# Softmax blocks of two attention branches turned by VectorE and carried through DRAM, both groups of a branch as one stream of steps

## The chip, the cores and the metric

The kernel runs on one core of a Trainium2 chip. The metric is the device time of one execution in microseconds (us). The engines of the core are named as the profile names them: PE (TensorE, matmuls), DVE (VectorE), ACT (ScalarE), POOL (GpSimd) and SP (SyncE, which here only issues DMAs). SPq and POOLq are the DMA queues that SP and POOL issue into. Each engine works through its own instructions in their order and waits, in place, for what the next one needs.

## What is computed

One decoder layer on 512 tokens of width 1024, in float32: h = RMSNorm(x), a projection of h into the columns of three token mixers and their gates, the mixers, their merge, an output projection and a last RMSNorm. Two of the three mixers are softmax attention with 8 heads of 64: forgetting attention (FoX) with a bias per head and key, and block-sparse attention (MoBA), which at this length sees all keys and adds an ALiBi bias. What the change touches is, per head:

```
logits = q @ k.T * scale + bias          # [512, 512], causal
p = softmax(logits, axis=-1)
out = p @ v
```

The third mixer is an mLSTM in chunked form, which has no softmax.

## The kernel before, in words

A float32 value is held as two float32r parts, `hi` and `lo`, and a product is made of three (in the attention: two) float32r matmuls. PE's order is written by hand. Its main stream are the projections: a `Unit` is 256 columns of a weight matrix, fetched in halves of 512 KB (`fetch`, tile `w_raw`, two buffers), split by ACT into `w_hi` and by DVE into `w_lo` (`load`), and used by 24 matmuls of 512 columns per half (lines 148 to 150). `UNIT` is the columns of one such unit, 48 matmuls.

The side work (attention, mLSTM) is a list of steps that `weave` puts between main matmuls: with `part` p and n steps, step i comes when i/n of p times the stage's main columns are done. The stages after the prologue and the first group's projections are:

- stage 2: projections of FoX group 1 (4 units), side: attention of FoX group 0;
- stage 3: projections of the mLSTM (8 units), side: attention of FoX group 1;
- stage 4: merge of FoX and projections of MoBA group 0 (10 units), side: mLSTM;
- stage 5: projections of MoBA group 1 (4 units), side: attention of MoBA group 0;
- stage 6: merge of the mLSTM (6 units), side: attention of MoBA group 1;
- then the merge of MoBA and the output projection.

A group has four heads, and a head two steps of each kind: an even step has the query blocks of 128 and 256 keys, an odd step those of 384 and 512. `scores` makes the logits on PE (lines 366, 367), takes the row maximum and adds the bias on DVE, exponentiates and scales on ACT (line 383, line 386). `transposes` turns each 128 x 128 block of the result by a PE matmul against the identity into PSUM (line 397) and splits it into `pth` and `ptl` (lines 65, 67). `values` multiplies by v (lines 415, 416). Before the change, step n of the list holds scores n, transposes n-1 and values n-2, and each group has a list of its own.

`make_k` copies both parts of k for each head to the other 64 partitions by two DMAs (tiles `sk_h`, `sk_l`). `row_bcast` spreads a row from DRAM over the partitions by a DMA (tile `bias`), and `add_mask` adds a causal mask on POOL. All these DMAs and the weight fetches are issued by SP in the order in which a scheduler puts them; the same scheduler orders ACT, DVE and POOL.

Of the kernel before, what the change touches and what calls it, by code (L numbers as in the profile page):

```python
# [15 lines left out]
P = 128  # L16
# [7 lines left out]
UC = 256  # L24
EPS = 1e-6
# [18 lines left out]
def hybrid_kernel(ctx: ExitStack, tc: tile.TileContext, x, norm_g, w_in, fox_b_f, mlstm_conv_w,  # L44
# [25 lines left out]

    class Unit:
# [107 lines left out]
    def weave(mains, total, side, part=1.0):  # L179
# [7 lines left out]
        for f in side[done:]:  # L187
# [4 lines left out]
    mask_q = const.tile([P, P], F32, name="mask_q")  # L192
    nc.gpsimd.memset(mask_q, 0.0)
    nc.gpsimd.affine_select(out=mask_q, in_=mask_q, pattern=[[-1, P]], compare_op=ALU.is_ge,
                            fill=NEG, base=0, channel_multiplier=1)
    mask_s = const.tile([P, P], F32, name="mask_s")
    nc.gpsimd.memset(mask_s, 0.0)
    nc.gpsimd.affine_select(out=mask_s, in_=mask_s, pattern=[[1, P]], compare_op=ALU.is_ge,
                            fill=NEG, base=0, channel_multiplier=-1)
    alibi = const.tile([P, S], F32, name="alibi")  # L200
    nc.gpsimd.iota(alibi, pattern=[[1, S]], base=P - S, channel_multiplier=-1,
                   allow_small_or_imprecise_dtypes=True)
    nc.gpsimd.affine_select(out=alibi, in_=alibi, pattern=[[-1, S]], compare_op=ALU.is_ge,
                            fill=NEG, base=S - P, channel_multiplier=1)
# [27 lines left out]
    w_f = const.tile([P, KD, 16], F32, name="w_f")  # L232

    ctx.enter_context(tc.manual_schedule(engines={mybir.EngineType.PE}))
    def gate_rows():
        w_fs = att.tile([P, KD, P], F32R, name="pth", bufs=2)
        nc.vector.tensor_scalar(w_fs, h_hi[:, :, S - P:S].bitcast(F32), 0.0, None, op0=ALU.mult)
# [3 lines left out]
        for k in range(KD):  # L241
            nc.tensor.matmul(fps, w_fs[:, k], hh(k), start=k == 0, stop=False)
            nc.tensor.matmul(fps, w_fs[:, k], hl(k), start=False, stop=k == KD - 1)
        pre, shifted, lg, ones_s = (new_bias() for _ in range(4))
        cum = ev.tile([P, S], F32, name="ev")
        nc.scalar.activation(pre, fps, AF.Copy)
# [43 lines left out]
    def make_k(src, scale, name):  # L290
        res = []
        for e in range(2):
# [6 lines left out]
            nc.sync.dma_start(th[o].bitcast(F32), th[r].bitcast(F32))  # L299
            nc.sync.dma_start(tl[o].bitcast(F32), tl[r].bitcast(F32))  # L300
# [14 lines left out]
    class Group:  # L315


        def __init__(self, g, cq, ck, cv, cz, bias, ys):
            self.g, self.bias, self.ys = g, bias, ys
            self.q, self.k, self.z = [], [], []  # L320
            self.u = {n: Unit(w_in_v, c + g * UC) for n, c in (("q", cq), ("k", ck), ("v", cv), ("z", cz))}
# [33 lines left out]
        def scores(self, n):  # L355
# [6 lines left out]
            for i in (2 * half, 2 * half + 1):  # L362
# [5 lines left out]
                pr = (att.tile([P, S], F32, name="pr", bufs=2) if half else  # L368
                      att.tile([P, 2 * P], F32, name="pr0", bufs=2))
# [19 lines left out]
        def transposes(self, n):  # L389
            half = n % 2  # L390
            pth = att.tile([P, NB, 2 * P], F32R, name="pth", bufs=2)
            ptl = att.tile([P, NB, 2 * P], F32R, name="ptl", bufs=2)
            for ii, pr in enumerate(self.pr.pop(n)):
                i = 2 * half + ii
                tp = ps_t.tile([P, S], F32, name="pt")
                for j in range(i + 1):
                    nc.tensor.transpose(tp[:, j * P:(j + 1) * P], pr[:, j * P:(j + 1) * P], ident)  # L397
                cs = slice(ii * P, ii * P + P)
                split(pth[:, 0:i + 1, cs], ptl[:, 0:i + 1, cs],
                      tp[:, :(i + 1) * P].rearrange("p (j q) -> p j q", q=P))  # L400
            self.pt[n] = pth, ptl

        def values(self, n):
# [6 lines left out]
            last = 2 * half + 1  # L410
            for j in range(last + 1):
# [3 lines left out]
                nc.tensor.matmul(reg, vj, pth[:, j, o0:], start=j == 0, stop=False)  # L415
                nc.tensor.matmul(reg, vj, ptl[:, j, o0:], start=False, stop=j == last)  # L416
# [13 lines left out]
        def side(self):  # L430
            self.pr, self.pt = {}, {}
            steps = []
            for n in range(10):
                if n < 8:
                    steps.append(lambda n=n: self.scores(n))
                if 0 < n < 9:
                    steps.append(lambda n=n: self.transposes(n - 1))
                if n > 1:
                    steps.append(lambda n=n: self.values(n - 2))
            return steps  # L440
# [6 lines left out]
    def add_mask(t, mask):  # L447
        d = new_bias()
        nc.gpsimd.tensor_tensor(d.rearrange("p (a b) -> p a b", b=P), t.rearrange("p (a b) -> p a b", b=P),
                                mask[:, None, :].to_broadcast([P, NB, P]), ALU.add)  # L450
        return d

    def fox_bias(h):
        whole = row_bcast(h)
        return whole, add_mask(whole, mask_q)

    def moba_bias(h):
        t = new_bias()
        nc.gpsimd.tensor_scalar(t, alibi, 2.0 ** -(h + 1), None, op0=ALU.mult)
# [41 lines left out]
    class Mlstm:  # L501
# [51 lines left out]
        def weights(self, m):  # L553
            h, j = divmod(m, NB)
            if j == 0:
                self.nmb = row_bcast(8 + h)
                self.nmd = add_mask(self.nmb, mask_s)
# [14 lines left out]
            wh = att.tile([P, S], F32R, name="pth", bufs=2)  # L572
# [411 lines left out]
```

## Time and profile before

| | us |
|---|---|
| median of 3 runs (605.6 to 606.15) | 605.93 |
| the profiled execution | 605.71 |
| its span, from the first to the last instruction | 603.8 |
| PE busy in it | 594.0 |
| DVE busy | 390.7 |
| ACT busy | 334.2 |
| POOL busy | 50.8 |

The span is 1.9 us shorter than the time of the same execution. Busy shares say which engine could be the limit; where the end is really set is read from the chain of waits and from the waits of each engine. A matmul's own duration is longer than the distance to the next one, because matmuls overlap; what a matmul costs on the path is the distance of their starts.

### The profile page before, as it was taken

The numbers are of one execution on the slowest core, as the hardware profiler recorded it, in microseconds if no ns is written. First come the engines' busy times: TensorE is split into PE (matmuls) and PEld (weight loads), VectorE is DVE, ScalarE is ACT, GpSimd is POOL, SyncE is SP. The second block draws the span as 40 slices with busy tenths as digits, with TensorE's granted clock in tenths as the row PEclk, the third lists the DMA queues.
The fourth block names the chain that finished last, engine by engine and source line by source line (L and its number), as shares of the span: only waits on it lengthen the run. The fifth ranks groups of instructions, "written<-read, shape, count | busy, mean of one in ns | idle before, by whom it ended". The sixth has DMA issues, their size and how long they took to land.

```text
span 603.8 us, 8372 instructions
## 1 busy us (share of the span) xinstructions
PE 594.0 (98%) x3109; PEld 509.2 (84%) x3109; DVE 390.7 (65%) x726; ACT 334.2 (55%) x616; POOL 50.8 (8%) x55
## 2 busy tenths in 40 slices
PE   8999999999999999999999999999999999999995
PEld 7988988888988988888898799888888888888884
DVE  6756667764477954856758856666655564356986
ACT  6555676675656545446536467666555433334555
POOL 3000100000000000010000400000000000001302
PEclk9999999999999999999999999999999999999999
DMA  7337432262142632234323642225322339833833
GB/s 249 104 92 176 113 98 78 87 192 88 53 123 71 174 97 79 69 97 113 88 71 95 197 128 71 71 71 148 96 71 71 87 92 342 206 111 76 142 97 139
DMA packets 59276, 69.75 MB, mean 116 GB/s; under 512 B 4972, under 2 KB 48008, under 8 KB 59236
## 3 DMA queue, kind: packets, MB, share of 16 engines
q1 hardware_dynamic: 56900, 64.76, 36.5%
q0 software_dynamic: 2176, 4.19, 4.3%
q8 instruction: 24, 0.39, 0.3%
q10 hardware_dynamic: 160, 0.27, 0.1%
q14 instruction: 16, 0.13, 0.1%
HBM read 61.68 MB, written 2.14 MB: 106 GB/s over the span
## 4 chain that ended last, share of the span: by engine, by line
PE 94%; DMA 2%; ACT 1%; DVE 1%; issue 1%; POOL 0%; SPq 0%; POOLq 0%; ACTq 0%
PE pj L148 22%; PE pj L150 22%; PE pj L149 22%; PE pj L167 4%; PE pj L169 4%; PE pj L168 4%; PE pt L397 3%; PE po L416 2%; PE sp L367 2%; PE sp L366 2%; PE po L415 2%; DMA x<-in_x_dram 1%; DMA w_raw<-in_w_out_dram 1%; DVE w_lo L94 1%; PE pt L865 1%; PE pt L864 1%
## 5 line engine op out<-in xcount | busy, mean ns | idle before, releaser
L148 PE MATMUL pj<-h_hi,w_hi 128*128 128x512 f32 x480 | 191.3, 399 | 0.5 <-DVE sq__3450 L285 0.3
L150 PE MATMUL pj<-h_hi,w_lo 128*128 128x512 f32 x480 | 187.5, 391 | 0.0
L149 PE MATMUL pj<-h_lo,w_hi 128*128 128x512 f32 x480 | 187.1, 390 | 0.0
L94 DVE TENSOR_TENSOR w_lo<-w_raw,w_hi 128x1024 fp32r<-128x1024 f32 x88 | 109.2, 1241 | 71.0 <-ACT w_hi L93 70.1
L93 ACT ACTIVATE w_hi<-w_raw 128x1024 fp32r<-128x1024 f32 x88 | 93.0, 1057 | 72.9 <-PE pj L149 46.8
L150 PEld LDWEIGHTS pj<-h_hi,w_lo 128*128 128x128 f32 x480 | 90.1, 188 | 19.7
L148 PEld LDWEIGHTS pj<-h_hi,w_hi 128*128 128x128 f32 x480 | 90.3, 188 | 18.1 <-issue 1.7
L149 PEld LDWEIGHTS pj<-h_lo,w_hi 128*128 128x128 f32 x480 | 90.4, 188 | 16.5
L167 PE MATMUL pj<-w_hi,h_hi 128*128 128x256 f32 x192 | 56.1, 292 | 0.5 <-ACT h_hi L65 0.5
L169 PE MATMUL pj<-w_hi,h_lo 128*128 128x256 f32 x192 | 55.0, 286 | 0.0
L168 PE MATMUL pj<-w_lo,h_hi 128*128 128x256 f32 x192 | 54.8, 285 | 0.0
L383 ACT ACTIVATE pr<-pr,nmax 128x128 f32<-128x128 f32 (+1 forms) x64 | 35.6, 557 | 27.8 <-DVE nmax L372 16.8
L67 DVE TENSOR_TENSOR ptl<-pt,pth 128x128 fp32r<-128x128 f32 (+1 forms) x64 | 29.3, 486 | 15.2 <-ACT pth L65 14.8
L167 PEld LDWEIGHTS pj<-w_hi,h_hi 128*128 128x128 f32 x192 | 37.2, 194 | 1.2 <-ACT h_hi L65 0.9
L148 PE MATMUL pj<-y_hi,w_hi 128*128 128x512 f32 x96 | 38.1, 397 | 0.0
L168 PEld LDWEIGHTS pj<-w_lo,h_hi 128*128 128x128 f32 x192 | 37.3, 194 | 0.3
L150 PE MATMUL pj<-y_hi,w_lo 128*128 128x512 f32 x96 | 37.5, 390 | 0.0
L149 PE MATMUL pj<-y_lo,w_hi 128*128 128x512 f32 x96 | 37.4, 389 | 0.0
L169 PEld LDWEIGHTS pj<-w_hi,h_lo 128*128 128x128 f32 x192 | 37.1, 193 | 0.2 <-DVE h_lo L67 0.2
L386 ACT ACTIVATE pr<-pr,rden 128x128 f32<-128x128 f32 (+1 forms) x64 | 33.7, 554 | 3.2 <-DVE rden L385 3.0
L65 ACT ACTIVATE pth<-pt 128x128 fp32r<-128x128 f32 (+1 forms) x64 | 24.9, 427 | 4.0 <-PE pt L397 3.9
L117 POOL DMA_DIRECT2D sum<-in_w_out_dram x8 | 9.8, 1225 | 163.4 <-DMA w_raw<-in_w_in_dram 113.2
(313 smaller groups left out, 905.5 us busy)
## 6 DMA issues: line engine op xcount, KB each, us to landing
w_raw<-in_w_in_dram SPq DMA_DIRECT2D x72, 512.0 KB, 3.9
w_raw<-in_w_branch_dram SPq DMA_DIRECT2D x12, 512.0 KB, 4.3
sum<-in_w_out_dram POOLq DMA_DIRECT2D x8, 512.0 KB, 7.1
bias<-scr SPq DMA_DIRECT2D x12, 256.0 KB, 3.1
sk_h<-sk_h SPq DMA_DIRECT2D x20, 128.0 KB, 2.9
sk_l<-sk_l SPq DMA_DIRECT2D x20, 128.0 KB, 6.0
x<-in_x_dram SPq DMA_DIRECT2D x4, 512.0 KB
xr<-in_x_dram SPq DMA_DIRECT2D x1, 2048.0 KB
```

The lines of the kernel that those rows point to most:

```text
L65: nc.scalar.activation(hi, src, AF.Copy, scale=scale)
L67: nc.vector.tensor_tensor(lo, src, hi.bitcast(F32), ALU.subtract)
L93: nc.scalar.activation(hi, raw, AF.Copy)
L94: (eng or nc.vector).tensor_tensor(lo, raw, hi.bitcast(F32), ALU.subtract)
L148: nc.tensor.matmul(bank, hi[:, kk, cs], act_hi(k), start=k == 0, stop=False)
L149: nc.tensor.matmul(bank, hi[:, kk, cs], act_lo(k), start=False, stop=False)
L150: nc.tensor.matmul(bank, lo[:, kk, cs], act_hi(k), start=False, stop=k == u.nk - 1)
L167: nc.tensor.matmul(reg, act_hi(k)[:, ts_], hi[:, kk], start=k == 0, stop=False)
L168: nc.tensor.matmul(reg, act_hi(k)[:, ts_], lo[:, kk], start=False, stop=False)
L169: nc.tensor.matmul(reg, act_lo(k)[:, ts_], hi[:, kk], start=False, stop=k == KD - 1)
L383: nc.scalar.activation(pr[:, :w], pr[:, :w], AF.Exp, bias=nmax, scale=-1.0, accum_out=den)
L386: nc.scalar.activation(pr[:, :w], pr[:, :w], AF.Copy, scale=rden)
```

## The change

`transposes` no longer uses PE. DVE turns the 32 x 32 blocks of each softmax block inside SBUF, one DMA writes the result of a step to DRAM, four DMAs read it back, one for each 32 partitions, so that the full 128 x 128 transpose arises, and the split into `pth` and `ptl` follows from SBUF, one ACT and one DVE instruction per step instead of two each. `values` reads its moving operand in runs of 32 columns. The two groups of a branch become one list of 16 steps that runs over two stages, with values n-4 instead of n-2 beside scores n; the `part` of stages 2, 3 and 5 changes. While this stream runs (`deep`), the weight fetches go to POOL's queue, and so do all copies of k and all row broadcasts, everywhere. The masks become `affine_select` on POOL, the ALiBi tile is made anew per head on POOL and scaled on DVE, and some tiles share buffers (`pr0` in one buffer, `pth0` and `pth1` in one each).

```diff
-            nc.sync.dma_start(raw, self.view[:, 4 * h:4 * h + 4, self.c0:self.c0 + UC])
+            (nc.gpsimd if deep[0] else nc.sync).dma_start(raw, self.view[:, 4 * h:4 * h + 4, self.c0:self.c0 + UC])
...
-            nc.sync.dma_start(th[o].bitcast(F32), th[r].bitcast(F32))
-            nc.sync.dma_start(tl[o].bitcast(F32), tl[r].bitcast(F32))
+            nc.gpsimd.dma_start(th[o].bitcast(F32), th[r].bitcast(F32))
+            nc.gpsimd.dma_start(tl[o].bitcast(F32), tl[r].bitcast(F32))
...
         def transposes(self, n):
             half = n % 2
-            pth = att.tile([P, NB, 2 * P], F32R, name="pth", bufs=2)
-            ptl = att.tile([P, NB, 2 * P], F32R, name="ptl", bufs=2)
-            for ii, pr in enumerate(self.pr.pop(n)):
-                i = 2 * half + ii
-                tp = ps_t.tile([P, S], F32, name="pt")
-                for j in range(i + 1):
-                    nc.tensor.transpose(tp[:, j * P:(j + 1) * P], pr[:, j * P:(j + 1) * P], ident)
-                cs = slice(ii * P, ii * P + P)
-                split(pth[:, 0:i + 1, cs], ptl[:, 0:i + 1, cs],
-                      tp[:, :(i + 1) * P].rearrange("p (j q) -> p j q", q=P))
+            c = (4 * half + 3) * Q
+            pth = att.tile([P, 4, c], F32R, name=f"pth{half}", bufs=1)
+            ptl = att.tile([P, 4, c], F32R, name=f"ptl{half}", bufs=2)
+            tr = att.tile([P, 4, c], F32, name=f"tr{half}")
+            at = 0
+            for pr in self.pr.pop(n):
+                nj = 2 * half + 1 + (at > 0)
+                nc.vector.transpose(tr[:, :, at:at + nj * Q].rearrange("p b (j k) -> p b j k", k=Q),
+                                    pr[:, :nj * P].rearrange("p (j b k) -> p b j k", b=4, k=Q))
+                at += nj * Q
+            raw = ptl.bitcast(F32)
+            turned = dram.tile([4, Q, 4, c], F32, name=f"turned{half}", bufs=2)
+            nc.sync.dma_start(turned.rearrange("a k b c -> (a k) b c"), tr)
+            for b in range(4):
+                nc.sync.dma_start(raw[b * Q:(b + 1) * Q], turned[:, :, b].rearrange("a k c -> k a c"))
+            nc.scalar.activation(pth, raw, AF.Copy)
+            nc.vector.tensor_tensor(ptl, raw, pth.bitcast(F32), ALU.subtract)
...
-                nc.tensor.matmul(reg, vj, pth[:, j, o0:], start=j == 0, stop=False)
-                nc.tensor.matmul(reg, vj, ptl[:, j, o0:], start=False, stop=j == last)
+                for t in (pth, ptl):
+                    if j == last:
+                        src = t[:, :, n0 + j * Q:n0 + (j + 1) * Q]
+                    else:
+                        src = bass.AP(t.tensor, t.offset + j * Q, [t.ap[0], [n0, 2], t.ap[1], [1, Q]])
+                    nc.tensor.matmul(reg, vj, src, start=j == 0 and t is pth, stop=j == last and t is ptl)
...
+    def attention(groups):
+        steps = [[], []]
+        for n in range(16 + DEEP):
+            at = steps[n > 7]
+            for late, name in ((0, "scores"), (1, "transposes"), (DEEP, "values")):
+                if 0 <= n - late < 16:
+                    g, i = divmod(n - late, 8)
+                    at.append(lambda f=getattr(groups[g], name), i=i: f(i))
+        return steps
...
-        nc.sync.dma_start(t, scr[row:row + 1, :].partition_broadcast(P))
+        nc.gpsimd.dma_start(t, scr[row:row + 1, :].partition_broadcast(P))
...
-    weave(fox[1].mains("vzqk"), 4 * UNIT, fox[0].side(), 0.85)
-    weave(mlstm.mains(m_order), 8 * UNIT, fox[1].side(), 0.6)
+    side_a, side_b = attention(fox), attention(moba)
+    weave(fox[1].mains("vzqk"), 4 * UNIT, side_a[0], 0.95)
+    weave(mlstm.mains(m_order), 8 * UNIT, side_a[1], 0.52)
+    deep[0] = False
     weave([merge_a.main()] + moba[0].mains("vqkz"), 10 * UNIT, mlstm.side(), 0.75)
-    weave(moba[1].mains("vzqk"), 4 * UNIT, moba[0].side(), 0.85)
-    weave([merge_c.main()], 6 * UNIT, moba[1].side())
+    deep[0] = True
+    weave(moba[1].mains("vzqk"), 4 * UNIT, side_b[0], 0.95)
+    weave([merge_c.main()], 6 * UNIT, side_b[1], 1.0)
```

How this moves instructions is shown at three places. The first is PE late in stage 3, before: the scores of the last head's odd step, the transposes of its even step, and the values that follow (`po`), with the main matmuls (`pj`) between them left out.

```order
L366 MATMUL sp_2046<-sk_h_1414,sq__1285 128x512
L367 MATMUL sp_2046<-sk_l_1415,sq__1285 128x512
...
L397 MATMUL pt_2074<-ident_87,pr0_1955 128x128
L397 MATMUL pt_2078<-ident_87,pr0_1966 128x128 x2
...
L415 MATMUL po_2015<-pth_1985,v_683 128x256
L416 MATMUL po_2015<-ptl_1986,v_683 128x256
```

The same place of PE in the changed kernel, from the last head's first values on (its even step reads `pth0`, its odd step `pth1`; of the nine and the six main matmuls ahead of them the last one stands).

```order
L358 MATMUL sp_1979<-sk_l_1355,sq__1199 128x512
...
L154 MATMUL pj_2102<-h_hi_98,w_lo_1947 128x512
L424 MATMUL po_2113<-pth0_1998,v_668 128x256
L424 MATMUL po_2113<-ptl0_1999,v_668 128x256
...
L154 MATMUL pj_2102<-h_hi_98,w_lo_1947 128x512
L424 MATMUL po_2113<-pth1_2047,v_668 128x256
L424 MATMUL po_2113<-ptl1_2048,v_668 128x256
```

No PE row is left between scores and values; from the last scores to the odd step's values PE now has 48 main matmuls and the values of four other steps, 8 + 4 + 8 + 4 matmuls.

The second place is SP at the same point of the changed kernel, where before it issued weights, rows and copies of k: `turned` is the block in DRAM, 0 for even and 1 for odd steps, and the last four rows are those of the last head.

```order
L399 DMA turned0_1827<-tr0_1824 128x384
L399 DMA turned1_1922<-tr1_1919 128x896
L401 DMA ptl0_1823<-turned0_1827 32x4x96 x4
L401 DMA ptl1_1918<-turned1_1922 32x4x224 x4
L399 DMA turned0_2003<-tr0_2000 128x384
L399 DMA turned1_2052<-tr1_2049 128x896
L401 DMA ptl0_1999<-turned0_2003 32x4x96 x4
L401 DMA ptl1_2048<-turned1_2052 32x4x224 x4
```

The reads of an even step's block stand behind the write of the next odd step's.

The third place is the queue that carries the copies of k from stage 2 to stage 3. Before, it is SP's:

```order
L444 DMA bias_1540<-scr_118 128x512
L81 DMA w_raw_1305<-in_w_in_dram 128x4x256
L81 DMA w_raw_1370<-in_w_in_dram 128x4x256
L299 DMA sk_h_1384<-sk_h_1384 64x512
L300 DMA sk_l_1385<-sk_l_1385 64x512
```

In the changed kernel the same work stands on POOL, with its own computation between:

```order
L452 DMA bias_1534<-scr_103 128x512
L85 DMA w_raw_1282<-in_w_in_dram 128x4x256
L290 DMA sk_h_1309<-sk_h_1309 64x512
L291 DMA sk_l_1310<-sk_l_1310 64x512
L290 DMA sk_h_1315<-sk_h_1315 64x512
L291 DMA sk_l_1316<-sk_l_1316 64x512
L458 AFFINE_SELECT bias_1536<-bias_1534 128x512
```

All six kinds keep their order; what changed is the engine that issues them. From stage 5 to stage 6 POOL has a `w_raw` fetch between the `sk_h` and the `sk_l` of the first head. POOL issues 50 of the 88 `w_raw` fetches.

## Rows read from the trace of the kernel before

**Rows 1.** The page: engines; the chain that ended last, by engine.

```profile
PE 594.0 (98%) x3109; PEld 509.2 (84%) x3109; DVE 390.7 (65%) x726; ACT 334.2 (55%) x616; POOL 50.8 (8%) x55
...
PE 94%; DMA 2%; ACT 1%; DVE 1%; issue 1%; POOL 0%; SPq 0%; POOLq 0%; ACTq 0%
```

**Rows 2.** All waits of PE: for whom, us, times, longest us.

```profile
PE sp L696 <- DVE idle L691: 1.5, 1, 1.5
PE pj L167 <- ACT h_hi L65: 0.5, 1, 0.5
PE pj L148 <- DVE sq__3450 L285: 0.3, 1, 0.3
```

**Rows 3.** The chain in order of time: start us, us, what.

```profile
69.74 0.33 PE pt L397 x3
...
485.42 0.76 PE pt L397 x7
```

**Rows 4.** Timeline of PE, start us, us: values, main matmuls.

```profile
108.83 0.28 PE L415 MATMUL po<-pth,v 128*128 128x256 f32 x1
...
109.72 0.45 PE L148 MATMUL pj<-h_hi,w_hi 128*128 128x512 f32 x1
...
119.09 0.39 PE L149 MATMUL pj<-h_lo,w_hi 128*128 128x512 f32 x1
...
125.44 0.39 PE L150 MATMUL pj<-h_hi,w_lo 128*128 128x512 f32 x1
```

**Rows 5.** Timeline of one odd softmax step, stage 3.

```profile
176.21 0.34 PE L366 MATMUL sp<-sk_h,sq__1285 128*128 128x384 f32 x1
...
179.28 1.22 ACT L386 ACTIVATE pr<-pr,rden 128x384 f32<-128x384 f32 x2
```

**Rows 6.** DMA issues: xcount, KB each, median us from issue to landing.

```profile
w_raw<-in_w_in_dram SPq DMA_DIRECT2D x72, 512.0 KB, 3.9
...
sum<-in_w_out_dram POOLq DMA_DIRECT2D x8, 512.0 KB, 7.1
bias<-scr SPq DMA_DIRECT2D x12, 256.0 KB, 3.1
sk_h<-sk_h SPq DMA_DIRECT2D x20, 128.0 KB, 2.9
sk_l<-sk_l SPq DMA_DIRECT2D x20, 128.0 KB, 6.0
...
out_dram<-xr SPq DMA_DIRECT2D x6, 256.0 KB, 2.0
```

**Rows 7.** All landings of w_raw; then POOL's DMAs of line 117.

```profile
DMA to landing us min/median/max: 3.3/3.9/9.5
...
L117 POOL DMA_DIRECT2D sum<-in_w_out_dram x8: 1203/1203/1378, 511.4 to 570.1; - x8
...
DMA to landing us min/median/max: 5.9/7.1/9.5
```

**Rows 8.** Timeline: a copy of k at the end of stage 2.

```profile
120.43 0.59 ACT L296 ACTIVATE sk_h<-pj 64x512 fp32r<-64x512 f32 x1 [0.77 <-PE pj L150]
...
121.76 0.46 SPq L300 DMA_DIRECT2D sk_l<-sk_l  x1
```

**Rows 9.** Groups by line: busy us, mean ns, idle before.

```profile
L94 DVE TENSOR_TENSOR w_lo<-w_raw,w_hi 128x1024 fp32r<-128x1024 f32 x88 | 109.2, 1241 | 71.0 <-ACT w_hi L93 70.1
L93 ACT ACTIVATE w_hi<-w_raw 128x1024 fp32r<-128x1024 f32 x88 | 93.0, 1057 | 72.9 <-PE pj L149 46.8
...
L67 DVE TENSOR_TENSOR ptl<-pt,pth 128x128 fp32r<-128x128 f32 (+1 forms) x64 | 29.3, 486 | 15.2 <-ACT pth L65 14.8
...
L622 DVE RECIPROCAL bias<-bias 128x512 f32<-128x512 f32 x1 | 3.4, 3353 | 1.3 <-ACT bias L621 1.3
```

**Rows 10.** Stages 2 and 3: PE, PEld, DVE, ACT, POOL busy, clock, DMA share.

```profile
63.00:125.00 62.00, 62.00 (x374) 54.92 (x374) 42.24 (x117) 42.74 (x91) 6.48 (x5) 1.00 0.34 101
125.00:192.00 67.00, 67.00 (x394) 59.00 (x393) 39.43 (x111) 41.59 (x92) 5.20 (x4) 1.00 0.35 102
```

More of the change, by code (lines that the diff above doesn't have):

```diff
@@ L24 @@
 UC = 256
+Q = 32
+DEEP = 4
 EPS = 1e-6
@@ L367, in scores @@
                 nc.tensor.matmul(sp[:, :w], qs, kl[:, :w], start=False, stop=True)
-                pr = (att.tile([P, S], F32, name="pr", bufs=2) if half else
-                      att.tile([P, 2 * P], F32, name="pr0", bufs=2))
+                if half:
+                    pr = att.tile([P, S], F32, name="pr", bufs=2)
+                else:
+                    if i == 0:
+                        pr0 = att.tile([P, 2, 2 * P], F32, name="pr0")
+                    pr = pr0[:, i]
                 nmax = small.tile([P, 1], F32, name="nmax")
@@ L410, in values @@
             last = 2 * half + 1
+            n0 = last * Q
             for j in range(last + 1):
@@ L428, in values, with add_mask @@
                     self.ys.append(y)
[L430 to L440, printed above, removed]
+    def attention(groups):
[7 more added lines that the diff above has]
+        return steps
     def row_bcast(row):
         t = new_bias()
-        nc.sync.dma_start(t, scr[row:row + 1, :].partition_broadcast(P))
+        nc.gpsimd.dma_start(t, scr[row:row + 1, :].partition_broadcast(P))
         return t
-    def add_mask(t, mask):
+    def add_mask(t, sign):
         d = new_bias()
-        nc.gpsimd.tensor_tensor(d.rearrange("p (a b) -> p a b", b=P), t.rearrange("p (a b) -> p a b", b=P),
-                                mask[:, None, :].to_broadcast([P, NB, P]), ALU.add)
+        nc.gpsimd.affine_select(out=d.rearrange("p (a b) -> p a b", b=P), in_=t.rearrange("p (a b) -> p a b", b=P),
+                                pattern=[[0, NB], [-sign, P]], compare_op=ALU.is_ge, fill=NEG, base=0,
+                                channel_multiplier=sign)
         return d
@@ L454, in fox_bias @@
         whole = row_bcast(h)
-        return whole, add_mask(whole, mask_q)
+        return whole, add_mask(whole, 1)
     def moba_bias(h):
         t = new_bias()
-        nc.gpsimd.tensor_scalar(t, alibi, 2.0 ** -(h + 1), None, op0=ALU.mult)
+        nc.gpsimd.iota(t, pattern=[[1, S]], base=P - S, channel_multiplier=-1,
+                       allow_small_or_imprecise_dtypes=True)
+        nc.gpsimd.affine_select(out=t, in_=t, pattern=[[-1, S]], compare_op=ALU.is_ge,
+                                fill=NEG, base=S - P, channel_multiplier=1)
+        nc.vector.tensor_scalar(t, t, 2.0 ** -(h + 1), None, op0=ALU.mult)
         return t, None
@@ L571, in weights @@
             nc.vector.tensor_tensor(w[:, :n], sp[:, :n], w[:, :n], ALU.mult)
-            wh = att.tile([P, S], F32R, name="pth", bufs=2)
-            wl = att.tile([P, S], F32R, name="ptl", bufs=2)
+            wh = att.tile([P, S], F32R, name=("pth1", "wh")[m % 2], bufs=(1, 1)[m % 2])
+            wl = att.tile([P, S], F32R, name="ptl1", bufs=2)
             split(wh[:, :n], wl[:, :n], w[:, :n])
@@ L581, in weights @@
             if j == NB - 1:
-                self.sums[h] = fold(self.sum, att.tile([P, S], F32R, name="sum_h"))
+                self.sums[h] = fold(self.sum, att.tile([P, S], F32R, name="tr1"))
         def values(self, m):
```

35 lines of the change are left out of this document (13 added, 22 removed).

## Prediction

> **What bounds the kernel now.** I read the page first: PE is busy for 98% of the span and makes up 94% of the chain that ended last [rows 1]. A busy PE alone proves little, so the waits of PE come next: in the whole run there are three, 2.3 us together, two of them in the prologue [rows 2]. From the first projection on PE runs from one matmul into the next, and every other engine's delays are hidden. In the timeline main matmuls of 512 columns start 0.227 us apart (28 of them from 119.09 to 125.44) though each lasts 0.39 [rows 4]. So a matmul taken off PE is worth the distance of starts that it filled, as long as nothing else begins to hold PE up. The kernel is PE's stream, and there are two questions: how much of it goes, and which waits come into it.
>
> **What is removed.** The chain in order of time has the transposes in pieces of three (0.33 us, even steps) and of seven (0.76 or 0.77 us, odd steps), the first at 69.74, the last at 485.42 [rows 3]. Each of 16 heads has one of either: 16 x (0.33 + 0.77) = 17.6 us. That is 0.11 us for each of 160 transposes, and they hide behind nothing, since PE has no gap beside them. I take 17.6.
>
> The Trainium skill weighs the same choice in "VectorE: DVE Perf Modes", section "The three transpose paths": it gives 390 ns to a 128 x 128 transpose on TensorE (2-byte type). By that figure the sum would be an estimated 62 us saved; the row shows 0.11 us apart, because the matmuls overlap, and the row decides.
>
> **What is added off PE.** Per head DVE turns 1280 columns; no row shows its transpose. Below it is bounded by the split of line 94, 1241 ns for 1024 columns, above by the slowest DVE row per column, the reciprocal of line 622, 3353 ns for 512 [rows 9]: 25 us or 134 us in all. The operation reads one operand and writes one, as cheap rows do, so I take 25. The splits that go with it shrink: 64 DVE instructions of 486 ns become 32 over 640 columns on average, at line 94's rate 0.78 each, so 31 becomes 25, and ACT likewise saves a little. Net DVE gains about 5 us per stage, and in stage 2 it is idle for 62.0 - 42.2 = 19.8 us [rows 10]: covered. At the upper bound it would not be (rivals).
>
> The DMAs carry each step's block out and back, 1280 x 512 bytes per head and direction, 21 MB in all, half of it in stages 2 and 3. Over their 129 us that is 81 GB/s more on 101, so their DMA share of 0.34 goes to an estimated 0.62 [rows 10]. No bandwidth bound; but landings may lengthen.
>
> The values now read runs of 32 columns. Their rows show only contiguous reads; an odd step's eight matmuls take 109.72 - 108.83 = 0.89 us, which is the rate of the main ones, and an even step's, with 768 columns in place of 1792, 0.38 [rows 4]. Lower bound of the change: nothing. Upper: the slowest rate per column that PE shows in these stages, that of the transposes, 0.11 us for 128 columns against 0.057, which on 16 x 1.27 = 20.3 us would be 19 more. Nearest is the contiguous read of the same type and size, so I take 0.
>
> **The trip through DRAM, and whom it makes wait.** Nobody but the values waits for it, and DEEP puts them four steps behind the scores. The tightest place is the last odd step of stage 3, where no scores follow to fill the gap: 48 main matmuls (10.9 us), the scores themselves (1792 columns, 0.79) and four steps of values (2 x 0.89 + 2 x 0.38) give 14.2 us from the scores to the values that need them. The chain in that time: scores to scaled softmax 4.3 us (176.21 to 179.28 + 1.22) [rows 5]; turning the last 512 columns 0.62 at line 94's rate; the write to DRAM 2.0 as a store of the output lands; four reads issued 0.46 apart [rows 8], the last 1.4 after the first; landing 2.9, as the copy of k [rows 6]; ACT 0.93 and DVE 1.09 for 896 columns at the rates of lines 93 and 94 [rows 9]. Sum 13.2, one us inside. With reads that land in 6.0 as `sk_l` does [rows 6] the values come 2.1 late; with 9.5, the slowest `w_raw` [rows 7], 5.6, and each handoff and each busy engine comes on top. I take 1 us and keep 0 and 6.6. At the same place of stage 6 the steps are farther apart and the margin is some 5 us: 0. Early and in the middle of the stream the distance is larger: main matmuls worth 86 of 512 columns and five steps of scores, 22.1 us, for the first step, and 26.3 for the first of group 1. SP's order makes an even step's reads wait for the next odd step's write; that adds one step, about 6.5 us, to a chain of 13: still inside.
>
> **What moves to POOL.** The copies of k decide two places. At the end of stage 2 the first head's copies can start when the last matmul of the bank is done; before, ACT starts at 120.43 and SP issues the second copy 1.33 us later [rows 8]. The first scores of stage 3 need it after 21 main matmuls and the values of one odd step, 5.7 us. On POOL an issue takes 1.2 us [rows 7], so the second copy starts at 1.85. If it lands in 2.9, PE does not wait; if in 7.1, as POOL's DMAs do [rows 6], it waits 3.3 us. From stage 5 to 6 a weight fetch stands between the two copies, another 1.2 us, against 24 main matmuls and the same values, 6.3 us: 0 or 3.8. Both ends together 0 to 7.1; I take 2, nearer to the SP row, because it is the same copy of 128 KB, while POOL's rows move 512 KB and add to what is there.
>
> The weights: each of two `w_raw` buffers goes through release, fetch, landing and 1.06 + 1.24 us of split. Call X the time from release to landing; a half can be had every (X + 2.3)/2 us. PE without its transposes uses one in 57.6 / 8 = 7.2 us in stage 2 and, by the main matmuls of the 67 us, 6.4 in stage 3. So X may be 12.1 and 10.5. POOL's median is 7.1 and its slowest 9.5 [rows 7]: covered, and two split halves lie ahead besides. What stands behind a blocked POOL instruction is every fetch and copy after it: `affine_select` waits for the row's landing (3.1 [rows 6]), which brings a slow fetch to 13.8 with its issue. Those are single ones, at most one per head; the two halves ahead absorb them. Masks and ALiBi tiles are off the path: 0.
>
> **Sum**, against the profiled execution's 605.7: -17.6 + 2 + 1 = -14.6, so 591.1; the median of the runs lies 0.2 above that execution, so I say 591. Its own range: 588 without a wait, 602 with both waits at their slow ends.
>
> **Rivals.**
> 1. *POOL supplies the weights too late.* If X is 13.8 throughout stages 2 and 3, a half costs (13.8 + 2.3)/2 = 8.05 us, 0.85 more than PE's in stage 2 (8 halves) and 1.65 in stage 3 (10): 23 us, less the two halves ahead, 13: 10 us, hence 601. For it: 50 fetches stand in one queue with waiting computation. Against: the measured 7.1. The Trainium skill, "SBUF — State Buffer", section "SBUF: two separate sides", speaks against the change here: a DMA from GpSimd's queue has its descriptors written by GpSimd and stalls while VectorE holds the shared port in a two-port operation, 620 ns becoming about 3100. By that figure an estimated X would be 9.6, still short of 10.5; no run here shows it so far. Chance 0.13.
> 2. *The other side: the trip is longer than the four steps.* Place: the reads on SP. With write and reads at 9.5 each the chain is 27.3 us; the distances are 22 to 26. Each window of four steps then loses their difference, 1 to 5 us; eight windows, about 25: 616. It decides from the point where the chain passes some 26 us, because 14.6/8 = 1.8 per window eats the gain. For it: DMA share nearly doubles and reads come in pieces of 384 or 896 bytes. Against: 13 us to spare. Chance 0.07.
> 3. *PE reads runs of 32 columns at half rate*: 591 + 19 = 610, the gain gone and more. Nothing in the trace speaks for it or excludes it. Chance 0.06.
> 4. *DVE turns at the reciprocal's rate*: 33.5 us per stage against 19.8 idle less the 4.4 that PE no longer spends, and similarly in the other three: about 50 us, 641. Chance 0.03.
> 5. *Many small waits at the stage boundaries* that use up the gain; the time unchanged. Chance 0.05.
>
> **How the numbers follow.** 0.66 is left for the forecast. A measurement of this kernel tells about 0.2% (1.2 us) from no change. Faster takes the forecast, nearly all of rival 1 and a little of 5: 0.79; same 0.04; slower, rivals 2 to 4 and what is left, 0.17. The range takes in the forecast's own ends and rival 1, 587.5 to 604, and leaves out 2 to 4.
>
> **What would show it.** Right: PE's chain without line 397 and its busy time about 17 us less; waits of PE for `sk_l` or `sk_h` at the first scores of stages 3 and 6, a few us in all; perhaps one for `ptl` in the last values of stage 3; values at 0.89 us per odd step; DVE's transposes near 0.6 us for 512 columns. Wrong: waits of PE for `w_hi` or `w_lo` (rival 1), for `pth` at every values step (rival 2), values stretched to 1.7 us (rival 3), DVE over 90% busy (rival 4). The forecast fails most easily by the landing of POOL's DMAs, which carries both the copies and the weights.

## The result and the profile after

The changed kernel takes 596.31 us (median of 4 executions, 594.71 to 958.02) against 605.76 (4 executions, 605.11 to 606.15); the ratio is 0.9836, with a 95% interval of 0.9813 to 0.9859. One of the four executions was disturbed (958.02, granted clock 0.558) and is not in the ratio; the median of the other three is 596.01. The profiled execution took 596.01 (its span is 594.2), 9.7 us less than the 605.71 of the one before, where 14.6 were forecast.

The page, engines and chain by engine; the rows answer to [rows 1].

```profile
PE 578.3 (97%) x2949; PEld 493.8 (83%) x2949; DVE 415.6 (70%) x766; ACT 333.5 (56%) x584; POOL 105.0 (18%) x159
...
PE 83%; ACT 4%; DVE 4%; DMA 4%; issue 3%; POOL 1%; SPq 0%; POOLq 0%; DVEq 0%; ACTq 0%
```

PE has lost 160 instructions and 15.7 us of busy time, but its share of the chain fell from 94 to 83%: PE now waits for others. Its waits by line, with total us, times and longest, against the three in [rows 2] (L357 and L358 are the matmuls of the scores, L424 those of the values, L152 to L154 main matmuls):

```profile
PE sp L358 <- DMA sk_l<-sk_l: 2.3, 2, 1.9
PE sp L710 <- DVE idle L705: 1.5, 1, 1.5
PE po L424 <- DVE ev L431: 1.2, 1, 1.2
PE pj L152 <- DVE sq__485 L276: 1.1, 1, 1.1
PE po L424 <- DVE ptl L403: 0.9, 1, 0.9
PE pj L171 <- ACT h_hi L67: 0.7, 1, 0.7
PE po L424 <- ACT pth L402: 0.7, 1, 0.7
PE pj L152 <- DVE sq__3451 L276: 0.3, 1, 0.3
```

No wait is for `w_hi` or `w_lo`, and none for the trip in the middle of the stream. What is new stands at four places: one in the prologue (`sq__485`), one at each first scores of a new group (`sk_l`, stage 3 and stage 6), and three in the last values of stage 3 (`ev`, `pth`, `ptl`). The timeline of PE (start us, us, what, and in brackets the idle time and who ended it) shows what they cost on the path, as the distance of starts:

```profile
43.59 0.39 PE L154 MATMUL pj<-h_hi,w_lo 128*128 128x512 f32 x1
45.05 0.47 PE L152 MATMUL pj<-h_hi,w_hi 128*128 128x512 f32 x1 [1.07 <-DVE sq__485 L276]
...
119.14 0.30 PE L357 MATMUL sp<-sk_h,sq__1149 128*128 128x128 f32 x1
119.86 0.30 PE L358 MATMUL sp<-sk_l,sq__1149 128*128 128x128 f32 x1 [0.42 <-DMA sk_l<-sk_l]
...
153.62 0.28 PE L424 MATMUL po<-pth,v 128*128 128x256 f32 x1
...
154.51 0.33 PE L171 MATMUL pj<-w_hi,h_hi 128*128 128x256 f32 x1
...
169.92 0.39 PE L154 MATMUL pj<-h_hi,w_lo 128*128 128x512 f32 x1
171.53 0.39 PE L424 MATMUL po<-pth,v 128*128 128x256 f32 x1 [1.22 <-DVE ev L431]
...
176.30 0.39 PE L154 MATMUL pj<-h_hi,w_lo 128*128 128x512 f32 x1
177.34 0.38 PE L424 MATMUL po<-pth,v 128*128 128x256 f32 x1 [0.65 <-ACT pth L402]
178.66 0.39 PE L424 MATMUL po<-ptl,v 128*128 128x256 f32 x1 [0.94 <-DVE ptl L403]
...
403.43 0.22 PE L357 MATMUL sp<-sk_h,sq__4091 128*128 128x128 f32 x1
405.50 0.30 PE L358 MATMUL sp<-sk_l,sq__4091 128*128 128x128 f32 x1 [1.86 <-DMA sk_l<-sk_l]
...
407.16 0.63 PE L154 MATMUL pj<-h_hi,w_lo 128*128 128x512 f32 x1
407.59 0.63 PE L152 MATMUL pj<-h_hi,w_hi 128*128 128x512 f32 x1
```

Less the normal distance, the prologue's wait costs 1.46 - 0.23 = 1.2, the first scores of stage 3 0.7 and of stage 6 2.0, and the end of stage 3 1.4 + 0.8 + 1.2 = 3.4 us. Behind the wait of stage 6 seven main matmuls, from 407.16 on, start 0.43 us apart in place of 0.23: another 1.4. That makes 8.7 us of waits, and -17.6 + 8.7 = -8.9 against a measured -9.7.

The remaining 0.8 does not come from a different start: over the profiles of this study PE's first main matmul starts between 8.7 and 9.8 us, but in these two at 9.40 (before) and 9.59 (after), and the last one at 596.09 and 586.62, so it is PE's stream between them that is 9.7 us shorter. Most of the 0.8 lies in the 17.6. Around an even step's transposes in the kernel before:

```profile
80.71 0.40 PE L150 MATMUL pj<-h_hi,w_lo 128*128 128x512 f32 x1
80.95 0.49 PE L397 MATMUL pt<-ident,pr 128*128 128x128 f32 x3
81.19 0.47 PE L148 MATMUL pj<-h_hi,w_hi 128*128 128x512 f32 x1
81.51 0.39 PE L149 MATMUL pj<-h_lo,w_hi 128*128 128x512 f32 x1
...
82.20 0.39 PE L149 MATMUL pj<-h_lo,w_hi 128*128 128x512 f32 x1
```

The three transposes fill 0.24 us to the next start, but the first main matmul behind them is followed only after 0.32. From 80.71 to 82.20 five main matmuls start, at 0.227 each 1.13 us, so the piece costs 0.36. Taken like this over all 32 pieces it is about 0.35 for an even and 0.78 for an odd step, 18.1 us in all, and -18.1 + 8.7 = -9.4; 0.3 us stay open. The values of an odd step, 153.62 to 154.51, take 0.89 us as before [rows 4].

### The profile page after: what moved, and what is told of

It is laid out like the page before. It is cut to its first block, busy times and chain, and to the rows that moved or that the text cites. A ratio compares the mean times of both kernels' runs of the same rounds, so it can differ in the third digit from the quotient of the medians.

```text
span 594.2 us, 8543 instructions
## 1 busy us (share of the span) xinstructions
PE 578.3 (97%) x2949; PEld 493.8 (83%) x2949; DVE 415.6 (70%) x766; ACT 333.5 (56%) x584; POOL 105.0 (18%) x159
## 4 chain that ended last, share of the span: by engine, by line
PE 83%; ACT 4%; DVE 4%; DMA 4%; issue 3%; POOL 1%; SPq 0%; POOLq 0%; DVEq 0%; ACTq 0%
PE pj L152 20%; PE pj L153 19%; PE pj L154 19%; PE pj L171 4%; PE pj L173 4%; PE pj L172 4%; PE po L424 3%; DMA sk_l<-sk_l 2%; PE sp L358 2%; ACT w_hi L97 2%; PE sp L357 1%; DMA x<-in_x_dram 1%; DVE w_lo L98 1%; DVE ptl L403 1%; DMA bias<-bias 1%
## 5 line engine op out<-in xcount | busy, mean ns | idle before, releaser
L152 PE MATMUL pj<-h_hi,w_hi 128*128 128x512 f32 x480 | 189.5, 395 | 1.4 <-DVE sq__485 L276 1.1
L154 PE MATMUL pj<-h_hi,w_lo 128*128 128x512 f32 x480 | 187.8, 391 | 0.0
L98 DVE TENSOR_TENSOR w_lo<-w_raw,w_hi 128x1024 fp32r<-128x1024 f32 x88 | 107.6, 1222 | 64.9 <-ACT w_hi L97 61.8
L152 PEld LDWEIGHTS pj<-h_hi,w_hi 128*128 128x128 f32 x480 | 90.7, 189 | 19.5 <-issue 2.2
L154 PEld LDWEIGHTS pj<-h_hi,w_lo 128*128 128x128 f32 x480 | 90.4, 188 | 19.4
L85 POOL DMA_DIRECT2D w_raw<-in_w_in_dram x44 | 33.8, 769 | 168.9 <-DVE w_lo L98 122.8
L152 PE MATMUL pj<-y_hi,w_hi 128*128 128x512 f32 x96 | 37.9, 395 | 0.0
L394 DVE STREAM_TRANSPOSE tr<-pr 128x128 f32<-128x128 f32 (+1 forms) x64 | 32.2, 506 | 7.6 <-ACT pr L381 6.1
L154 PE MATMUL pj<-y_hi,w_lo 128*128 128x512 f32 x96 | 37.4, 390 | 0.0
L403 DVE TENSOR_TENSOR ptl<-ptl,pth 128x384 fp32r<-128x384 f32 (+1 forms) x32 | 26.7, 833 | 7.0 <-ACT pth L402 6.8
```

Of the source, the lines that this page charges most:

```text
L85: (nc.gpsimd if deep[0] else nc.sync).dma_start(raw, self.view[:, 4 * h:4 * h + 4, self.c0:self.c0 + UC])
L98: (eng or nc.vector).tensor_tensor(lo, raw, hi.bitcast(F32), ALU.subtract)
L152: nc.tensor.matmul(bank, hi[:, kk, cs], act_hi(k), start=k == 0, stop=False)
L154: nc.tensor.matmul(bank, lo[:, kk, cs], act_hi(k), start=False, stop=k == u.nk - 1)
L403: nc.vector.tensor_tensor(ptl, raw, pth.bitcast(F32), ALU.subtract)
```

## The experiments

All are the changed kernel with the edit shown. Times are medians; the kernel before, run beside them, took 604.6 to 605.2. "A" in the expectations was my theory after the first reading: POOL's queue order and DMAs make the copies of k late.

**e1_k_sp.** In `make_k`, both copies:

```diff
-            nc.gpsimd.dma_start(th[o].bitcast(F32), th[r].bitcast(F32))
+            nc.sync.dma_start(th[o].bitcast(F32), th[r].bitcast(F32))
```

> The copies of k are issued by SP again, all else as changed. Theory A (the copies are late because of POOL's queue: issued behind a weight fetch, 0.78 us, and landing in 5 us where SP's took 2.9): PE's two waits for sk_l (0.7 and 2.0 us) and the half clock behind the second (1.7 us) go, 596.0 - 4.4 = 591.6 us. Rival B (the copies land late because the DMA engines carry the trip of the softmax blocks, whoever issues them): landing stays near 5 us, a wait of 1 us or more stays at the first scores of stage 6, 594 us or more.

595.56 us, ratio 0.9837 (0.9814 to 0.986): no better than the changed kernel. The copies land a little earlier (median 4.0 and 3.9 us in place of 4.9 and 5.0), and the wait at stage 6 falls from 1.9 to 1.1 us. So POOL is a part of the lateness and not most of it; A was too simple. Its 2.9 us was also the figure of `sk_h` alone: `sk_l`, for which PE waits, had 6.0 on SP before the change [rows 6]. Rival B's signs came (a wait of over 1 us, 594 us or more), but the cause that it names, the trip's traffic, is tested by e4.

**e2_w_sp.** In `fetch`, `(nc.gpsimd if deep[0] else nc.sync)` becomes `nc.sync`.

> All weight fetches are issued by SP, the copies of k and the rows stay on POOL. Theory A: no fetch stands between the copies of k any more, so sk_l starts 0.8 us earlier at stage 6: the wait there falls from 2.0 to about 1.2, and the prologue's 1.0 us goes; if SP held nothing else this would be 593 us or less. Rival C (SP's order decides: a fetch waits there for a free buffer, up to 12 us on POOL in the changed kernel, and the reads and writes of the trip stand behind it): PE waits for pth or ptl at many values steps, 1 us or more each over 28 steps, 610 us or more.

614.35 us, ratio 1.0152 (1.0122 to 1.0183), slower than the kernel before. SP's own longest wait in total (first fence) and those of PE at the values (second):

```profile
SPq L85 <- DVE w_lo L98: 244.5, 57, 12.5
```

```profile
PE po L424 <- ACT pth L402: 4.5, 4, 1.8
PE po L424 <- DVE ptl L403: 3.7, 4, 1.5
PE po L424 <- DMA w_raw<-in_w_in_dram: 3.0, 1, 3.0
```

A fetch stands on SP until DVE has released its buffer, up to 8.3 us while a stream runs (the 12.5 of the row is in stage 4, and stands in the changed kernel too), and the trip's reads and writes stand behind it. C was right in kind, though PE waits nine times at the values and not at nearly every step: sending the fetches to POOL is what lets the trip through, worth 18 us here. One thing of A held: the prologue's wait fell from 1.1 to 0.2 us, so that one came from the fetch moved to POOL.

**e3_part.** `side_a[1], 0.52` becomes `0.65` (the part of stage 3).

> The part of stage 3 goes from 0.52 to 0.65, so the last four values stand 25% farther apart. Theory A (the three waits of PE at the end of stage 3, 1.38 + 0.81 + 1.21 = 3.4 us, are the last steps following each other too closely, with no scores between): they go or fall below 0.5 us in all, 592.6 us. Rival B (what is late there is the trip itself, and the steps in the middle of the stage have the same chain): waits of 2 us or more stay, 594.5 us or more.

594.27 us, ratio 0.9828 (0.9806 to 0.985). The waits of the last values are now 1.5 for `ptl`, 0.8 for `ev` and 0.2 for `pth`: 2.5 us in place of 2.8. More room between the steps did not remove them; A's figure of 0.5 is refuted. At the first scores of stage 3 a wait of 1.3 us for `sk_h` is new.

**e4_no_trip.** The trip through DRAM is left out, so only the 32 x 32 blocks are turned. After `tr` is made:

```diff
-            raw = ptl.bitcast(F32)
-            turned = dram.tile([4, Q, 4, c], F32, name=f"turned{half}", bufs=2)
-            nc.sync.dma_start(turned.rearrange("a k b c -> (a k) b c"), tr)
-            for b in range(4):
-                nc.sync.dma_start(raw[b * Q:(b + 1) * Q], turned[:, :, b].rearrange("a k c -> k a c"))
-            nc.scalar.activation(pth, raw, AF.Copy)
-            nc.vector.tensor_tensor(ptl, raw, pth.bitcast(F32), ALU.subtract)
+            nc.scalar.activation(pth, tr, AF.Copy)
+            nc.vector.tensor_tensor(ptl, tr, pth.bitcast(F32), ALU.subtract)
```

> The trip through DRAM is left out: pth and ptl are split straight from what DVE turned, so only the 32 x 32 blocks are turned and the output is not the reference's; 21 MB of DMA traffic go, the order on PE stays. Rival B (traffic and length of the trip cause the waits): the waits at the end of stage 3 go and the copies of k land in about 3 us, so their waits and the half clock go too: 596.0 - 3.4 - 4.4 = 588 us. Theory A (order of POOL, ACT and DVE): the copies land as late as before and the wait of 2.0 us with its half clock stays; of the waits at the end of stage 3 the one for the evacuation of po (1.4 us) stays: 592 to 594 us.

594.14 us, ratio 0.9817 (0.98 to 0.9833), an interval that overlaps that of the changed kernel: without 21 MB of traffic and without the trip's latency little is won. The waits of PE that bear on it:

```profile
PE po L419 <- DVE ev L426: 3.5, 3, 2.1
PE sp L358 <- DMA sk_l<-sk_l: 1.8, 2, 1.6
```

With 0.5 us for `sk_h` the waits for k are 2.3 us, as in the changed kernel; the waits for `pth` and `ptl` are gone, but those for `ev` have grown from 1.2 to 3.5, so the values wait no less in all (3.5 in place of 2.8). B falls as the cause of the lost time: PE waits as long without the trip and its traffic. What is left is the order in which ACT and DVE do their work. In the changed kernel ACT shows it at both places (start us, us, what, idle before and who ended it):

```profile
174.62 0.60 ACT L430 ACTIVATE ev<-po 64x512 f32<-64x512 f32 x1 [1.75 <-PE po L424]
175.82 1.06 ACT L97 ACTIVATE w_hi<-w_raw 128x1024 fp32r<-128x1024 f32 x1 [0.60 <-PE pj L153]
176.78 0.50 ACT L402 ACTIVATE pth<-ptl 128x384 fp32r<-128x384 f32 x1
...
393.83 0.59 ACT L275 ACTIVATE sq__4139<-pj 64x512 fp32r<-64x512 f32 x1 [2.53 <-PE sp L358]
...
396.89 1.05 ACT L97 ACTIVATE w_hi<-w_raw 128x1024 fp32r<-128x1024 f32 x1
397.96 0.59 ACT L287 ACTIVATE sk_h<-pj 64x512 fp32r<-64x512 f32 x1
```

At 174.62 the split for the next values (`pth`, 176.78) stands behind the emptying of a bank that waits for PE's own values of the step before. Its data had been there for four us: the four reads of that block were issued before 170.4 and landed within 2.4 us. At 393.83 ACT has stood 2.53 us for the last scores of the old group, which free the buffer of q; the softmax of that step and a weight split follow, and `sk_h` comes at 397.96.

**e5_pe_turn.** PE turns the blocks again, in the changed order and with the changed queues:

```diff
-            pth = att.tile([P, 4, c], F32R, name=f"pth{half}", bufs=1)
...
+            pth = att.tile([P, c], F32R, name=f"pth{half}", bufs=2)
...
-                nc.vector.transpose(tr[:, :, at:at + nj * Q].rearrange("p b (j k) -> p b j k", k=Q),
-                                    pr[:, :nj * P].rearrange("p (j b k) -> p b j k", b=4, k=Q))
-                at += nj * Q
...
+                tp = ps_t.tile([P, S], F32, name="pt")
+                for j in range(nj):
+                    nc.tensor.transpose(tp[:, j * P:(j + 1) * P], pr[:, j * P:(j + 1) * P], ident)
+                split(pth[:, at:at + nj * P], ptl[:, at:at + nj * P], tp[:, :nj * P])
+                at += nj * P
```

> The softmax blocks are turned by PE again, 160 transposes against the identity, with everything else of the change kept: the list of steps over two stages with values four steps behind, POOL's queue for weights, rows and copies of k, the masks. Theory A (the turn off PE is worth 18 us, and the waits come from POOL's queue and from the order of ACT and DVE at the stage borders, whoever turns): the waits of 1.1 us in the prologue and of 2 to 4 us at the first scores of stages 3 and 6 stay, 611 to 614 us, which is 6 us or more above the kernel before. Rival E (the waits come from what DVE and the trip do now): without them they vanish and the time is that of the kernel before, 605 to 608 us.

The trip goes too, and `values` reads contiguous columns again. 607.59 us, ratio 1.0034 (1.002 to 1.0047). All the rest of the change without its core costs 2 us. The waits of PE that bear on it:

```profile
PE sp L358 <- DMA sk_l<-sk_l: 1.3, 1, 1.3
PE pj L152 <- DVE sq__485 L276: 1.0, 1, 1.0
```

A and E each hold in half: the wait for k at stage 6 and that of the prologue stay, whoever turns; that for k at stage 3 and those at the end of stage 3 are gone, so they belong to what ACT and DVE do for the new way. One thing is not kept apart here: the edit also gives `pth` two buffers in place of one. In the changed kernel ACT stands 6.6 us in all for PE before the splits `pth`, at eight of 32; the one at 176.78 is not among them. Turning off PE is worth 607.6 - 596.3 = 11.3 us net: the 18.1 less the 3.4 of the tail, the 1.4 of low clock (no stretch of it here) and about 1 at the copies of k would be 12.3.

**e6_po2.** `self.po = ps_o.tile([P, S], F32, name="po")` becomes `ps_t.tile([P, S], F32, name="pt")`.

> The result of the values gets the two PSUM banks of pt, which the attention no longer uses, in place of the one bank po; one line. Theory A (a step's values wait until ACT and DVE have emptied the bank of the step before, behind the split of the next block): the wait of PE for DVE's ev (1.4 us) goes, and the other two of the tail (0.8 and 1.2 us) move little: 594.6 us. Rival (that wait only hides the late blocks behind it): the same time is waited for pth or ptl instead, 596 us.

594.8 us, ratio 0.9814 (0.9791 to 0.9838), as A expected: the wait for `ev` is gone, 0.9 for `ptl` and 0.6 for `pth` stay. The interval overlaps that of the changed kernel, so the time alone decides nothing; the missing wait does.

**e7_parts.** The parts of stages 2 and 5 back to 0.85, that of stage 3 0.65.

> The parts of stages 2 and 5 go back to 0.85 as they were before the change (from 0.95), that of stage 3 is 0.65. Theory A (the first copies of k are late because ACT and DVE still work on the last softmax step of the stage when the bank of k is done: sk_l is issued 3.2 us after it, 1.5 us before the change): with the last step of stages 2 and 5 some 4 us earlier, sk_h and sk_l are made at once, the copies are issued 1.5 us earlier and the wait at stage 6 falls from 2.0 to 0.5 us or less, the one at stage 3 goes: about 591.5 us with the gain of the wider tail. Rival A2 (it is the 5 us that a copy issued by POOL takes to land): the wait falls by less than 0.7 us, 593.5 us or more.

603.01 us, ratio 0.9964 (0.9952 to 0.9977): most of the gain is lost, the opposite of what I expected. PE waits 8.3 us for `sk_h` at the two borders, 6.3 of them at stage 3. The timeline of POOL there:

```profile
115.88 0.77 POOL L85 DMA_DIRECT2D w_raw<-in_w_in_dram  x1 [1.38 <-DVE w_lo L98]
116.65 0.55 POOL L290 DMA_DIRECT2D sk_h<-sk_h  x1
```

The copy stands behind a fetch that waits for DVE, and then lands after 7.7 us. As I read the timelines (no run takes it apart): with all steps done earlier, PE runs straight from the bank of k to the first scores, and the last values, their emptying and their split now fall on ACT and DVE in just that time. Moving the stage's steps moves the collision, it does not take it away.

**e8_all and e9_four.** e8: copies of k on SP, the parts of e7, the bank of e6, and `deep` set only ahead of stage 2. e9: the same with 0.95 kept in stages 2 and 5.

> All four edits that single runs point to: copies of k on SP, the parts of the run e7_parts, two banks for the values, and weight fetches on POOL only from stage 2 on (not in the prologue, where the fetch on POOL collides with the copy of the gate rows and costs 1.1 us). Theory A: every wait found so far is taken away at its place, 596.0 - 4.4 - 3.4 - 1.1 = 587 us, and the profile shows less than 1.5 us of waits of PE after the prologue. Rival (the waits move to the next place in ACT's or DVE's order): 590 us or more, with new waits named in the profile.

> As the run e8_all, but stages 2 and 5 keep the part of 0.95: copies of k on SP, part of stage 3 0.65, two banks for the values, weight fetches on POOL only from stage 2 on. If the part of 0.85 was what cost e7_parts and e8_all their time (the first scores of the next stage then come while ACT and DVE still hold the block, the bank of the values and the split that stand ahead of k), the gains of the single runs add: 596.3 - 1.0 (prologue) - 1 to 2 (copies) - 2.0 (tail) - 1.5 (bank) = 590 to 591 us. Rival (all these waits are one chain through ACT and DVE, so what one edit saves the next one saves again): 593 us or more.

600.05 us (0.9914, 0.9894 to 0.9935) and 595.24 (0.9839, 0.9814 to 0.9865). In e8 PE waits 2.9 us for `sk_l`, 2.2 for `ptl` and 1.7 for `pth`, in e9 still 2.0, 1.5 and 1.4. The gains of single edits do not add. That fits the rival, one chain through ACT and DVE behind all the waits; the chain itself was not followed in these two.

**e10_kq.** The order of the projections in the second group, in the list of units and in the stages:

```diff
-    weave(fox[1].mains("vzqk"), 4 * UNIT, side_a[0], 0.95)
+    weave(fox[1].mains("vzkq"), 4 * UNIT, side_a[0], 0.95)
...
-    weave(moba[1].mains("vzqk"), 4 * UNIT, side_b[0], 0.95)
+    weave(moba[1].mains("vzkq"), 4 * UNIT, side_b[0], 0.95)
```

> In stages 2 and 5 the projection of k comes before that of q, so that the copies of k have a unit of 11 us more before the first scores of the next stage; all else as changed. Theory L (what PE waits for there is the landing of the copy, 5 us, after a late issue): the two waits (0.7 and 2.0 us, and the half clock of 1.7 us where it follows) go, 592 to 593.6 us. Theory O (what is late there is ACT's and DVE's order, whatever they evacuate): PE now waits for sq by 1 us or more at these two places, 595 us or more.

590.35 us (590.1 to 591.54), ratio 0.9759 (0.974 to 0.9778), below the changed kernel by more than both intervals. All waits of PE of 0.5 us and more:

```profile
PE sp L710 <- DVE idle L705: 1.5, 1, 1.5
PE po L424 <- DVE ev L431: 1.5, 1, 1.5
PE pt L780 <- DVE x L771: 1.2, 1, 1.2
PE pj L152 <- DVE sq__485 L276: 1.1, 1, 1.1
PE po L424 <- DVE ptl L403: 0.9, 1, 0.9
PE po L424 <- ACT pth L402: 0.7, 1, 0.7
```

Nobody waits for k or q at the borders. L holds, O falls: q is just as late on ACT and DVE, but it needs no copy, so it is in time. At the two borders the copies on POOL still take 2.4 to 6.2 us to land; they now have a unit's time for it. The gain, 6.0 us, is more than the 4.1 of the two waits and the half clock in the profile of the changed kernel. Between the two profiles (5.9 us) 1.8 of it comes from the prologue, which the edit does not touch: PE's 26th main matmul starts at 14.14 in place of 15.94. From there on the stream is 4.3 us shorter, 0.9 at the first scores of stage 3, 3.7 at those of stage 6 and -0.3 in the tail.

**e11_kq_three.** e10 with the part of 0.65, the two banks, and `deep` from stage 2 on.

> The projection of k before that of q in stages 2 and 5, with the part of stage 3 at 0.65, two banks for the values, and weight fetches on POOL only from stage 2 on; the copies of k stay on POOL. Theory L: no wait at the borders, none over 1 us in the tail, none in the prologue: 588 to 590 us, below the runs of single edits. Theory O: a wait for sq or pth of 1 us or more at the borders, 592 us or more.

594.65 us (0.9823, 0.9801 to 0.9844): 4 us worse than e10. The prologue's wait is gone, but a new one of 2.0 us for DVE's `nmax` stands at the second scores of stage 2, with matmuls at half rate behind it, and the tail waits 1.5 and 1.4, with half rate behind them too. L was right at the borders; the sum was wrong.

**e12_kq_po2.** e10 with the two banks alone.

> The projection of k before that of q in stages 2 and 5, and two banks for the values; the parts and the queues as changed. In the run e10_kq the three waits at the end of stage 3 are left, 1.5 us for the emptied bank and 0.8 and 1.2 us for pth and ptl. If the bank is a wait of its own, 590.35 - 1.5 = 588.9 us, and the two others stay. Rival (the values that no longer wait for the bank wait for the split that stands behind it on ACT and DVE): 590 us or more, the sum of the waits at the end of stage 3 stays above 3 us.

589.98 us (589.74 to 590.53), ratio 0.9747 (0.9733 to 0.9761). The wait for `ev` is gone, 0.9 and 0.6 for `ptl` and `pth` stay, and no stretch of half rate is left between the prologue and the last product. It is the fastest version found, 15 us below the kernel before; its interval overlaps that of e10, so what the second bank adds is not settled.

## Why the prediction came out as it did

The direction, the mechanism and the range held; the gain was 9.5 us (medians) where 14.9 were forecast. By its steps:

- **Removed, 17.6 us: right in kind, 0.5 too low.** Line 397 is gone from PE, and nothing fills its place. I took the 0.33 and 0.77 from the chain, where they are the lengths of its pieces, and called them distances of starts; by starts, with the slower ones behind each piece, it is 18.1, and the ledger closes to 0.3.
- **DVE's turn: right in kind.** I took 25 us in all. The page's group (busy us, mean ns, then the idle time before):

```profile
L394 DVE STREAM_TRANSPOSE tr<-pr 128x128 f32<-128x128 f32 (+1 forms) x64 | 32.2, 506 | 7.6 <-ACT pr L381 6.1
```

  It is 32.2 us, and DVE is busy for 48.5 of the 62 us of stage 2 (42.2 in [rows 10]). Rival 4 falls.
- **Values in runs of 32 columns at nothing: right.** 0.89 us per odd step; rival 3 falls.
- **The weights on POOL: right.** No wait for them. The issues of DMAs, with count, KB and median us from issue to landing, against [rows 6]:

```profile
w_raw<-in_w_in_dram POOLq DMA_DIRECT2D x44, 512.0 KB, 4.5
w_raw<-in_w_in_dram SPq DMA_DIRECT2D x28, 512.0 KB, 3.7
...
sk_h<-sk_h POOLq DMA_DIRECT2D x20, 128.0 KB, 4.9
sk_l<-sk_l POOLq DMA_DIRECT2D x20, 128.0 KB, 5.0
```

  POOL's fetch lands in 4.5 us, not in the 7.1 of the accumulating DMAs I took as bound. Rival 1 falls; e2 shows that the move was needed. The page "SBUF — State Buffer" of the Trainium skill, section "SBUF: two separate sides", let POOL's DMAs be held up by DVE's two-port operations, by which I had estimated 2.5 us more. With DVE busy as above, POOL's fetches land 0.8 us later than SP's (3.7); whether any of that is this stall no run here shows.
- **The trip four steps behind, 1 us at the end of stage 3: mis-sized, 3.4, and for another reason.** I summed the chain of one step as if ACT and DVE were free at each handoff and asked only how DMAs land. e4 leaves the trip out, and the values wait as long in all. The values of the last steps wait for the bank `po`, and for splits that stand on ACT and DVE behind the emptying of that bank and behind weight splits. The sentence "each handoff and each busy engine comes on top" was right and should have had a price; the 6.6 that I kept as an upper end is one us more than the 5.6 that I had worked out, and no row gives it. At the end of stage 6 I had 0, and there is no wait. Rival 2 falls: there is no such wait in the middle.
- **The copies of k, 2 us: mis-sized, 2.7 and 1.4 of half clock behind it.** I let the copy start when the bank of k is done. At stage 6 `sk_h` comes off ACT at 398.55 and `sk_l` is issued at 400.26, behind ACT's 2.53 us for the last scores, a softmax step, a weight split and a fetch on POOL; the landing of 5.1 us then ends at 405.37. The kernel before had no such step at the border: there ACT stood idle for the bank of k, as in [rows 8]. Nor did I ask what fills the DMA engines there. They are busy for 0.90 of the time from 400 to 405 us (0.42 in the five before), and for 0.91 in e4, which has no trip: so it is mainly the copies themselves and the weight fetches between them. What the copies would take without those fetches no run here shows. e10 gives the copy more time and changes nothing else, and these waits are gone. That it comes to 590.35 us, nearly the 591 of the forecast, is luck: it has nothing for k where I had 2, 3.7 in the tail where I had 1, and 1.2 in the prologue where I had 0.
- **Left out: the prologue, 1.2 us.** I priced POOL's fetches in the stages and not those ahead of them. There one is issued just ahead of the copy of the gate rows (`bias<-bias`), which DVE then gets 4.1 us after its issue; in e2, with fetches on SP, it is 3.2, and the wait is 0.2 us in place of 1.1.

The errors add to 0.7 + 1.4 + 2.4 + 1.2 - 0.5 = 5.2 us of a forecast that was 4.9 too low for this execution; the rest is the 0.3 that stays open.

## What to carry to other kernels

When work is taken off the engine that is the bound, price it by distances of starts, the slower ones behind it included (that part came within 0.5 us), and then walk through each handoff of the new chain on the helper engines in their own order: what stands ahead of it there, and for whom that waits. At the borders between stages the lateness was cured here by giving the copy more time, that is by producing first what needs a DMA, and not by another queue or by moving all steps. Gains of single edits did not add here; edits that touch the same engines' order have to be run together.

## What the hardware showed unexpectedly

TensorE ran at half rate for a while after some of its waits. In the changed kernel it was held 2.0 us at 403.43 with the granted clock at full; from 407.16 main matmuls start 0.43 us apart, and the windows show the granted clock fall (the columns are those of [rows 10]; the last two are the busy share of the DMA engines and GB/s):

```profile
400.00:405.00 5.00, 3.65 (x17) 2.82 (x15) 4.71 (x6) 3.30 (x6) 3.18 (x6) 1.00 0.90 222
405.00:410.00 5.00, 4.50 (x15) 3.70 (x16) 2.67 (x9) 1.97 (x7) 1.57 (x3) 0.70 1.06 266
407.00:408.00 1.00, 1.00 (x4) 0.73 (x3) 0.94 (x3) 0.30 (x1) 0.00 (x0) 0.50 1.02 229
```

Of the two levels, 1.2 and 2.4 GHz, 0.50 is the lower one; the 0.70 is a mean over both. In the profiles of all runs there are ten such stretches between the prologue and the last product, and their main matmuls lose 0.8 to 2.3 us in each. Each follows a hold of about 2 us or more, or two or three shorter ones close together; but not every such hold has one behind it (2.17 us in e3_part, 2.25 in e4_no_trip and 3.07 in e8_all have none). What decides between the two no run here shows. So a wait of 2 us on PE has a price of 2 to 4 us here, which no row of the kernel before could show, since it never waited that long after the prologue.
